# Spreading the next layer's transposes over features and token groups, and splitting rows of w2 where they are used, in a two-layer hybrid mixer

## The chip, the cores and the metric

One core of a Trainium2 chip runs the whole program in one launch. The metric is the device time of that launch in microseconds (us), from the first to the last instruction with what lies around it, as a median over runs.

## What is computed

Two layers over 512 latent tokens (X, four tiles of 128) and 256 context tokens (C, two tiles). Each layer mixes tokens and then runs a gated feed-forward network:

```python
    h = x * (1.0 + sc1) + sh1
    proj = h @ w_in[l]
    ...
    x = layer_norm(DEEPNORM_ALPHA * x + g1 * (mix @ w_out), ln1g, ln1b)
    h = x * (1.0 + sc2) + sh2
    ffn = (jax.nn.silu(h @ w1) * (h @ w3)) @ w2
    return layer_norm(DEEPNORM_ALPHA * x + g2 * ffn, ln2g, ln2b)
```

The model width D is 1024 (8 blocks of 128, called k), the feed-forward width 2816 (22 blocks of 128, called features or ft). Context tokens go through layer 0 only; layer 1 still needs their normed projections. The modulation vectors (sh, sc, g) come from `silu(c) @ w_mod[l]`.

## The kernel before

**Arithmetic.** Every fp32 operand is kept as two fp32r parts. `split` (L168, L169) writes the high part by a cast on ScalarE (ACT) and the low part by a subtraction on VectorE (DVE). `mm3` (L172 to L174) makes one product out of three matmuls.

**Weights.** A list `plan` holds every weight tile in the order of use. `getw(key, la)` returns a tile and starts the loads of the `la` tiles behind it. A plan entry made by `add` calls `wload` (L178 on): it takes one of four raw buffers (S4), one of five split buffers (W8), starts the load on SP's queue (L186), and puts the split, and for layer 1's w2 a multiplication by the gate g2 (L189), at a priority 100 steps early. An entry made by `addraw` only loads.

**Order.** A scheduler orders the instructions of each engine when the program is built, by priority and by its own estimate of when operands are ready. Each engine then works strictly through its list.

**Feed-forward, down-projection** (`wout_ffn`, from L1190). Layer 0 runs two passes over the 22 features: C0, C1, X0 in pass 0, and X1, X2, X3 in pass 1; layer 1 has one pass over the four X tiles. `feat(pi, ft)` fetches the feature's activations (`y<-yd`, L1203), gets the w2 tile and splits y into u. `mm` then multiplies, for each token tile and each half of 512 columns, so that a feature of pass 1 is 18 matmuls 128x512 with six accumulators. `fill(1)` takes one step of layer 1's modulation products (`mods`, L274: w_mod tiles of 512 KB times `sst`) in each feature.

**The hook.** At feature 6 of pass 1, `hook(res, 0)` first empties the filler down to two generators, then runs `make_h` for the context tiles over all eight k: two transposes into a PSUM buffer `ps` (L360), an activation that applies the modulation and writes `y` (L362), and the split of `y` into `hT` (u). `hook(res, 1)` does the same for X0 and X1 behind the second tile of the last features. The PS pool has four one-bank buffers; in pass 1 two are accumulators and one holds the modulation products, so one is left for the transposes.

**In-projection of layer 1** (`inproj`, L412 on). Three token groups, (C0, C1), (X0, X1), (X2, X3): the first with 160 columns, the others with 416. For each k it splits w_in, makes h of that k and multiplies. Behind a group, `make_h` of the next group's first two k (`NPRE`) follows. The accumulators are PD buffers, which also hold layer 0's last accumulators until `ffn_last` (L1021) has read them.

**Layer 1's step from up to down.** The up-projection (L1187) ends with feature 21, whose split weights wa, wb and further forms take W8 buffers too, as do the first w2 tiles.

The names in rows: `w` a W8 tile, `s` an S4 tile, `u` a split operand, `y` an unsplit one, `f` a full-width tile, `ps` and `pd` the PSUM pools PS and PD, `ident` the identity.

Of the kernel before, what the change touches and what calls it, by code (L numbers as in the profile page):

```python
# [17 lines left out]
P = 128  # L18
# [72 lines left out]
def hybrid_kernel(ctx: ExitStack, tc: tile.TileContext, out: bass.AP, g: dict):  # L91
# [233 lines left out]
    def getw(key, la=2):  # L325
        i = index[key]
        ahead(i + 1 + la)
        return ready.pop(key)
# [3 lines left out]
    def add(key, src, shape, gate=None):  # L332
        index[key] = len(plan)
        plan.append((key, lambda: wload(src, shape, gate)))
# [77 lines left out]
    def inproj(l, groups, make_h):  # L412
# [6 lines left out]
        for gi, grp in enumerate(groups):  # L419
# [8 lines left out]
            for k in range(KD):  # L428
# [7 lines left out]
                for (st, t), a in zip(grp, acc):  # L436
                    h = st.hT[k]
                    ts_ = slice(t * P, (t + 1) * P)
                    mm3(a[:, c0:NA], h[:, 0, ts_], h[:, 1, ts_], w[0][:, k % 2], w[1][:, k % 2], k == 0, k == KD - 1)
            if gi + 1 < len(groups):  # L440
                for k in range(NPRE):
                    make_h(k, groups[gi + 1])

            for i, ((st, t), ac) in enumerate(zip(grp, acc)):
# [560 lines left out]

    NCONV, NLAST = 3, 4
    DVE_LN = ((1, 1), (2, 0), (2, 1))
    gbox = []

    def ffn_last(l, st, t, accs, ya, gb, bc, final, res, tail):  # L1010

# [76 lines left out]
    def wout_ffn(l, streams, final, hook=None):  # L1088
# [103 lines left out]
        def feat(pi, ft):  # L1192

            tiles = passes[pi]
            n = len(tiles) * P
            y = Y(n)
            i = 0
            while i < len(tiles):
                st, t = tiles[i]
                c, m = col[(st.s, t)], 1  # L1200
                while i + m < len(tiles) and col[(tiles[i + m][0].s, tiles[i + m][1])] == c + m * P:
                    m += 1
                nc.sync.dma_start(out=y[:, i * P:(i + m) * P], in_=yd[l][ft][:, c:c + m * P])  # L1203
                i += m
            w2 = getw(("2", l, pi, ft), 1)
            d = U(F32R, 2 * n).rearrange("p (a b) -> p a b", a=2)
            split(d[:, 0], d[:, 1], y)
            return d, w2
# [34 lines left out]
        gb = {}  # L1243
        for ft in range(NCONV, NF):
            if ft == NF - 4:
                gb = {st.s: gates(l, 1, st.s, FT) for st in streams}
                if final:
                    gbox.append(gb[0])
            cur = unit(ft, wn)
            next(cur)  # L1250
            if ft + 1 < NF:
                wn = up_forms(l, ft + 1)
            if prev:
                next(prev)
            next(cur)
            if prev:
                next(prev)
            next(cur)
            if prev:
                run(prev)  # L1260
            prev = cur
# [12 lines left out]
        for pi, tiles in enumerate(passes):  # L1274
# [15 lines left out]
            for ft in range(NF - NLAST):  # L1290
                d = nx
                if ft + 1 < NF - NLAST:
                    nx = feat(pi, ft + 1)
                for i in range(len(tiles)):
                    mm(i, [ft], [d])
                if not final and (pi == 0 or ft < 6):
                    fill(1)
                if hook and pi and ft == 6:
                    hook(res, 0)
                if ft == 8:  # L1300
                    for st, t in tiles:
                        y = FT()
                        nc.sync.dma_start(out=y, in_=rd[l][st.jt + t])
                        G_.tensor_tensor(out=y, in0=y, in1=bc[0], op=ALU.mult)  # L1304
                        G_.tensor_tensor(out=y, in0=y, in1=bc[1], op=ALU.add)
                        ya.append(y)
            fts = list(range(NF - NLAST, NF))
            ds = [feat(pi, ft) for ft in fts]
            for i, (st, t) in enumerate(tiles):
                mm(i, fts, ds)  # L1310
                if i == len(tiles) - 1 and pi + 1 < len(passes):
                    nx = feat(pi + 1, 0)
                ffn_last(l, st, t, accs[i], ya[i], gb[st.s], lb, final, res, final and i == len(tiles) - 1)
                if hook and pi and i == 1:
                    hook(res, 1)
        return res


# [3 lines left out]
    for l in range(2):  # L1322
# [26 lines left out]
                    addraw((n, l, ft), src, (KD, P))  # L1349
        for pi in range(2 if l == 0 else 1):  # L1350
            for ft in range(NF):
                add(("2", l, pi, ft), g["w_ffn2"][l][ft * P:(ft + 1) * P, :], (D,), gbox if l == 1 else None)

    phase("inp")
    toks = {(st.s, t): I(n=D) for st, t in allg}
# [17 lines left out]
    pars = [params(0), params(1)]  # L1373
    AB = {}
    made = set()
    NPRE = 2

    def make_h(k, grp):
        if (k, grp[0]) in made:
            return  # L1380
        made.add((k, grp[0]))
        for st in (X, C):
            ts_ = [t for s_, t in grp if s_ is st]
            if not ts_:
                continue
            if len(st.hT) <= k:
                st.hT += st.alloc(1 if st.s == 0 else 2)
            sl = slice(ts_[0] * P, (ts_[-1] + 1) * P)
            to_hT([toks[(st.s, t)] for t in ts_], lambda kk: st.hT[kk][:, :, sl], *AB[st.s], ks=[k])
# [8 lines left out]
            for p in pars:  # L1398
                next(p)

    def hook(res, i):

        grp = HOOK[i]
        if not AB:
            while len(filler) > 2:
                fill(1)
            for s_ in (C, X):
                made.clear()
                AB[s_.s] = fold(1, 0, s_.s, PV[:, 0, PG2:PG2 + 8], PV[:, 0, PB2:PB2 + 8])
                s_.hT = []  # L1410
        toks.update(res)
        for k in range(KD):
            make_h(k, grp)

    HOOK = [allg[4:6], allg[0:2]]
    for st in (X, C):
        st.hT = []
    AB.update({st.s: (modT[:, 0, 1, st.s], modT[:, 0, 0, st.s]) for st in (X, C)})
# [96 lines left out]
```

## Time and profile before

| | us |
|---|---|
| median of 3 runs | 1672.93 |
| lowest and highest run | 1671.89, 1675.65 |
| the profiled execution's own time | 1668.66 |
| its span, first to last instruction | 1666.9 |
| PE (TensorE) busy | 1572.3 (94%) |
| DVE busy | 1045.8 (63%) |
| ACT busy | 769.3 (46%) |
| POOL (GpSimd) busy | 260.6 (16%) |
| mean granted clock of TensorE, share of full | 0.984 |

A timeline row has the start, the duration, the engine (SPq is SP's queue), the program line, the operation, what is written from what, how many instructions of the kind follow one another, and in brackets the idle time before with what ended it. Each engine's idle time can be asked for any stretch; PE is the one that fills the span, so its idle rows are the places where another engine sets the time. PEclk of a window is the mean granted clock as a share of 2.4 GHz; 0.5 is the level of 1.2 GHz. Places used below, in us of the span: layer 0's pass 0, 752 to 882; pass 1, 882 to 1004; layer 1's in-projection, 1004 to 1036; layer 1's up-projection until 1519 and its down-projection from there.

### The profile page before, as it was taken

The page shows a single profiled execution, that of the slowest core. Times are in us where ns is not written, and L with a number is a line of the kernel's source. Part 1 is how long each engine was busy: PE and PEld are TensorE (multiplying, and loading weights), DVE is VectorE, ACT ScalarE, POOL GpSimd, SP SyncE. Part 2 cuts the span into 40 slices and gives each one's busy share as a digit, 9 for nine tenths or more (in the row PEclk, how much of TensorE's full clock was granted, in tenths as well). Part 3 has the DMA queues.
Part 4 walks back from the last instruction along what each step waited for, and adds up shares of the span by engine and source line. Part 5 has one row for each costly group of instructions (what it writes and reads, how often), then busy time and mean ns, then how long its engine had stood idle before and what let it go on. Part 6 is the DMA issues. An engine that isn't in the chain of part 4 may idle for free.

```text
span 1666.9 us, 23834 instructions
## 1 busy us (share of the span) xinstructions
PE 1572.3 (94%) x9129; PEld 1358.9 (82%) x9129; DVE 1045.8 (63%) x1591; ACT 769.3 (46%) x1371; POOL 260.6 (16%) x322
## 2 busy tenths in 40 slices
PE   6999889999999999999999798989999899998997
PEld 3856778888899999997766487879988899997786
DVE  1443676876766666664544437677857778886835
ACT  2521675884633434344232516368845445554220
POOL 0213011330000000000305005433311000001402
PEclk9999999999999999999999799999999999999999
DMA  9566114128322333449876726411156244457321
GB/s 327 178 218 202 39 39 140 46 81 279 110 82 93 94 95 101 130 133 338 315 257 226 222 67 200 145 33 39 39 176 197 76 127 127 127 177 266 119 82 58
DMA packets 180502, 241.80 MB, mean 145 GB/s; under 512 B 10874, under 2 KB 127468, under 8 KB 180388
## 3 DMA queue, kind: packets, MB, share of 16 engines
q1 hardware_dynamic: 180388, 240.28, 44.8%
q8 instruction: 72, 1.18, 0.3%
q14 instruction: 42, 0.34, 0.1%
HBM read 215.30 MB, written 24.94 MB: 144 GB/s over the span
## 4 chain that ended last, share of the span: by engine, by line
PE 81%; DVE 8%; DMA 4%; ACT 4%; issue 2%; SPq 0%; POOL 0%; POOLq 0%; DVEq 0%; ACTq 0%
PE pd L1187 21%; PE pd L172 10%; PE pd L173 10%; PE pd L174 10%; PE ps L172 5%; PE ps L173 5%; PE ps L174 5%; PE ps L1187 4%; PE ps L274 3%; PE ps L731 3%; PE ps L715 2%; DVE w L169 2%; DVE u L169 2%; DMA u<-in_w_mod_dram 1%; DMA s<-in_w_ffn_dram 1%
## 5 line engine op out<-in xcount | busy, mean ns | idle before, releaser
L168 ACT CAST w<-s 128x1024 fp32r<-128x1024 f32 (+3 forms) x285 | 292.7, 1031 | 473.0 <-PE pd L1187 141.2
L169 DVE TENSOR_TENSOR w<-s,w 128x1024 fp32r<-128x1024 f32 (+3 forms) x285 | 352.5, 1244 | 195.8 <-ACT w L168 195.7
L1187 PE MATMUL pd<-u,w 128*128 128x256 f32 (+1 forms) x1938 | 295.4, 308 | 19.0 <-DVE w L169 14.3
L1187 PEld LDWEIGHTS pd<-u,w 128*128 128x128 f32 x1938 | 282.7, 191 | 25.2 <-DVE w L169 15.8
L172 PE MATMUL pd<-w,u 128*128 128x512 f32 (+5 forms) x728 | 277.9, 383 | 8.3 <-DVE u L169 3.6
L173 PE MATMUL pd<-w,u 128*128 128x512 f32 (+5 forms) x728 | 274.3, 377 | 1.7 <-DVE w L169 1.7
L174 PE MATMUL pd<-w,u 128*128 128x512 f32 (+5 forms) x728 | 272.9, 376 | 0.0
L172 PEld LDWEIGHTS pd<-w,u 128*128 128x128 f32 x728 | 140.3, 193 | 54.6 <-issue 16.3
L173 PEld LDWEIGHTS pd<-w,u 128*128 128x128 f32 x728 | 140.3, 193 | 29.3 <-issue 5.9
L174 PEld LDWEIGHTS pd<-w,u 128*128 128x128 f32 x728 | 140.2, 193 | 27.2 <-issue 4.2
L168 ACT CAST u<-y 128x512 fp32r<-128x512 f32 (+2 forms) x178 | 94.2, 546 | 61.5 <-DMA y<-yd 28.4
L169 DVE TENSOR_TENSOR u<-y,u 128x512 fp32r<-128x512 f32 (+2 forms) x118 | 77.7, 679 | 63.0 <-ACT u L168 61.8
L169 POOL TENSOR_TENSOR u<-y,u 128x512 fp32r<-128x512 f32 (+1 forms) x60 | 78.9, 1323 | 225.5 <-ACT u L168 203.2
L172 PE MATMUL ps<-u,w 128*128 128x256 f32 (+2 forms) x288 | 92.1, 328 | 1.8 <-DVE modT L300 1.1
L174 PE MATMUL ps<-u,w 128*128 128x256 f32 (+2 forms) x288 | 93.5, 327 | 0.0
L173 PE MATMUL ps<-u,w 128*128 128x256 f32 (+2 forms) x288 | 93.3, 326 | 0.1
L172 PE MATMUL ps<-w,u 128*128 128x512 f32 (+1 forms) x208 | 81.2, 398 | 5.6 <-DVE u L169 4.7
L169 DVE TENSOR_TENSOR u<-ps,u 128x512 fp32r<-128x512 f32 (+2 forms) x106 | 66.7, 654 | 28.8 <-ACT u L168 27.8
L173 PE MATMUL ps<-w,u 128*128 128x512 f32 (+1 forms) x208 | 82.0, 395 | 1.4 <-DVE w L169 1.4
L174 PE MATMUL ps<-w,u 128*128 128x512 f32 (+1 forms) x208 | 81.4, 393 | 0.0
L1304 POOL TENSOR_TENSOR f<-f,f 128x1024 f32<-128x1024 f32 x10 | 25.8, 2598 | 333.5 <-DMA f<-rd 254.4
L1187 PE MATMUL ps<-u,w 128*128 128x384 f32 (+1 forms) x456 | 75.3, 313 | 0.0
(250 smaller groups left out, 2579.5 us busy)
## 6 DMA issues: line engine op xcount, KB each, us to landing
s<-in_w_ffn_dram SPq DMA_DIRECT2D x154, 512.0 KB
s<-in_w_out_dram SPq DMA_DIRECT2D x50, 512.0 KB
u<-in_w_mod_dram SPq DMA_DIRECT2D x48, 512.0 KB
s<-in_w_mod_dram SPq DMA_DIRECT2D x48, 512.0 KB
s<-in_w_in_dram SPq DMA_DIRECT2D x16, 512.0 KB
yd<-f SPq DMA_DIRECT2D x19, 384.0 KB
y<-yd SPq DMA_DIRECT2D x88, 64.0 KB
y<-yd SPq DMA_DIRECT2D x22, 256.0 KB
```

The lines of the kernel that those rows point to most:

```text
L168: A_.copy(out=hi, in_=src)
L169: (eng or V_).tensor_tensor(out=lo, in0=src, in1=f(hi), op=ALU.subtract)
L172: T_.matmul(ps, lhsT=ll, rhs=rh, start=start, stop=False)
L173: T_.matmul(ps, lhsT=lh, rhs=rl, start=False, stop=False)
L174: T_.matmul(ps, lhsT=lh, rhs=rh, start=False, stop=stop)
L274: T_.matmul(ps[32 * j:32 * j + 32, :n], lhsT=sst[:, k, :], rhs=ws[j // 2][:, (j % 2) * n:(j % 2 + 1) * n], start=(k == 0), stop=(k == KD - ...
L715: T_.transpose(pt[:, o:o + P], es[t2][:, k * P:(k + 1) * P], ident)
L731: T_.matmul(av[:, 0:256], lhsT=vt[k][:, h, :], rhs=pts[k // 2][:, a, (k % 2) * 256:(k % 2 + 1) * 256], start=(k == 0 and a == 1), stop=(k ...
L1187: T_.matmul(ps, lhsT=A[u][:, k], rhs=B[k][:, v], start=first and k == 0 and i == 0, stop=last and k == 3 and i == 2, skip_group_check=True)
L1304: G_.tensor_tensor(out=y, in0=y, in1=bc[0], op=ALU.mult)
```

## The change

1. **w2 raw.** w2's plan entries become raw loads, two tiles ahead (one for the last two features). `feat` takes the W8 buffer itself, multiplies by the gate where it is layer 1, and splits, at normal priority. `gbox` goes.
2. **Hook per feature.** In features 5 to 12 of pass 1 the hook is called with k = ft - 5 and makes that k of C0, C1 and X0: a pair of transposes for C and a single one for X0. The call behind the second tile goes.
3. **Filler.** It takes a step in a feature only while more than one generator is left, so that the last one, `mods(1, (4, 5))`, keeps its other steps for layer 1.
4. **In-projection.** h of the next group is made inside the loop over k, one k each; `made` remembers k and tile, so X1 is made alone (X0 being there) and the pair (X2, X3) behind the multiplications of the same k.

```diff
--- before.py
+++ after.py
@@ -437,8 +437,7 @@
                     h = st.hT[k]
                     ts_ = slice(t * P, (t + 1) * P)
                     mm3(a[:, c0:NA], h[:, 0, ts_], h[:, 1, ts_], w[0][:, k % 2], w[1][:, k % 2], k == 0, k == KD - 1)
-            if gi + 1 < len(groups):
-                for k in range(NPRE):
+                if gi + 1 < len(groups):
                     make_h(k, groups[gi + 1])
 
             for i, ((st, t), ac) in enumerate(zip(grp, acc)):
@@ -1005,7 +1004,6 @@
 
     NCONV, NLAST = 3, 4
     DVE_LN = ((1, 1), (2, 0), (2, 1))
-    gbox = []
 
     def ffn_last(l, st, t, accs, ya, gb, bc, final, res, tail):
 
@@ -1202,7 +1200,12 @@
                     m += 1
                 nc.sync.dma_start(out=y[:, i * P:(i + m) * P], in_=yd[l][ft][:, c:c + m * P])
                 i += m
-            w2 = getw(("2", l, pi, ft), 1)
+            s2 = getw(("2", l, pi, ft), 2 if ft < NF - 2 else 1)
+            w2 = W8()
+            if final:
+                V_.tensor_tensor(out=s2, in0=s2, in1=gb[0], op=ALU.mult)
+            split(w2[:, 0, :D], w2[:, 1, :D], s2)
+            w2 = w2[:, 0, :D], w2[:, 1, :D]
             d = U(F32R, 2 * n).rearrange("p (a b) -> p a b", a=2)
             split(d[:, 0], d[:, 1], y)
             return d, w2
@@ -1243,9 +1246,7 @@
         gb = {}
         for ft in range(NCONV, NF):
             if ft == NF - 4:
-                gb = {st.s: gates(l, 1, st.s, FT) for st in streams}
-                if final:
-                    gbox.append(gb[0])
+                gb.update({st.s: gates(l, 1, st.s, FT) for st in streams})
             cur = unit(ft, wn)
             next(cur)
             if ft + 1 < NF:
@@ -1293,10 +1294,11 @@
                     nx = feat(pi, ft + 1)
                 for i in range(len(tiles)):
                     mm(i, [ft], [d])
-                if not final and (pi == 0 or ft < 6):
-                    fill(1)
-                if hook and pi and ft == 6:
-                    hook(res, 0)
+                if hook:
+                    if len(filler) > 1:
+                        fill(1)
+                    if pi and 5 <= ft < 5 + KD:
+                        hook(res, ft - 5)
                 if ft == 8:
                     for st, t in tiles:
                         y = FT()
@@ -1311,8 +1313,6 @@
                 if i == len(tiles) - 1 and pi + 1 < len(passes):
                     nx = feat(pi + 1, 0)
                 ffn_last(l, st, t, accs[i], ya[i], gb[st.s], lb, final, res, final and i == len(tiles) - 1)
-                if hook and pi and i == 1:
-                    hook(res, 1)
         return res
 
 
@@ -1349,7 +1349,7 @@
                     addraw((n, l, ft), src, (KD, P))
         for pi in range(2 if l == 0 else 1):
             for ft in range(NF):
-                add(("2", l, pi, ft), g["w_ffn2"][l][ft * P:(ft + 1) * P, :], (D,), gbox if l == 1 else None)
+                addraw(("2", l, pi, ft), g["w_ffn2"][l][ft * P:(ft + 1) * P, :].rearrange("p (a n) -> p a n", a=2), (2, 512))
 
     phase("inp")
     toks = {(st.s, t): I(n=D) for st, t in allg}
@@ -1373,14 +1373,10 @@
     pars = [params(0), params(1)]
     AB = {}
     made = set()
-    NPRE = 2
-
     def make_h(k, grp):
-        if (k, grp[0]) in made:
-            return
-        made.add((k, grp[0]))
         for st in (X, C):
-            ts_ = [t for s_, t in grp if s_ is st]
+            ts_ = [t for s_, t in grp if s_ is st and (k, s_.s, t) not in made]
+            made.update((k, st.s, t) for t in ts_)
             if not ts_:
                 continue
             if len(st.hT) <= k:
@@ -1398,21 +1394,18 @@
             for p in pars:
                 next(p)
 
-    def hook(res, i):
-
-        grp = HOOK[i]
+    def hook(res, k):
+
         if not AB:
-            while len(filler) > 2:
+            while len(filler) > 1:
                 fill(1)
             for s_ in (C, X):
                 made.clear()
                 AB[s_.s] = fold(1, 0, s_.s, PV[:, 0, PG2:PG2 + 8], PV[:, 0, PB2:PB2 + 8])
                 s_.hT = []
         toks.update(res)
-        for k in range(KD):
-            make_h(k, grp)
-
-    HOOK = [allg[4:6], allg[0:2]]
+        make_h(k, allg[4:6] + allg[0:1])
+
     for st in (X, C):
         st.hT = []
     AB.update({st.s: (modT[:, 0, 1, st.s], modT[:, 0, 0, st.s]) for st in (X, C)})
```

Up to PE's instruction of about 740 us the two programs' orders are the same on every engine. Three places differ in what matters here.

PE, pass 1 before, the hook: rows of its list from the last matmul of feature 6 (`w_1265`) to the first of feature 7 (`w_1271`); `f_7403` and `f_7407` are the normed context tiles, `f_7411` is X0.

```order
L174 MATMUL pd_7935<-w_1265_8143,u_8184 128x512
L360 MATMUL ps_8244<-ident,f_7403 128x128
L360 MATMUL ps_8244<-ident,f_7407 128x128
L360 MATMUL ps_8251<-ident,f_7403 128x128
L360 MATMUL ps_8251<-ident,f_7407 128x128
L360 MATMUL ps_8259<-ident,f_7403 128x128
L360 MATMUL ps_8259<-ident,f_7407 128x128
L360 MATMUL ps_8266<-ident,f_7403 128x128
L360 MATMUL ps_8266<-ident,f_7407 128x128
L360 MATMUL ps_8722<-ident,f_7411 128x128
L172 MATMUL ps_7932<-w_1271_8180,u_8281 128x512
```

PE, pass 1 of the change: the last matmul of one feature, five transposes in three PSUM tiles, and the first matmul of the next.

```order
L174 MATMUL pd_7934<-w_1257_8111,u_8114 128x512
L360 MATMUL ps_8151<-ident,f_7402 128x128
L360 MATMUL ps_8151<-ident,f_7406 128x128
L360 MATMUL ps_8188<-ident,f_7410 128x128
L360 MATMUL ps_8194<-ident,f_7402 128x128
L360 MATMUL ps_8194<-ident,f_7406 128x128
L172 MATMUL ps_7931<-w_1269_8163,u_8166 128x512
L173 MATMUL ps_7931<-w_1269_8163,u_8166 128x512
```

The long run of context pairs at one place is gone. In its stead, behind eight features, stand by turns one transpose (X0) and five (a context pair, X0 of the next k, its context pair); the five stand four times.

ACT, pass 1 of the change, beside those five transposes; `w_1310` is a later feature's w2, `u_8166` the high part of the feature that PE takes next.

```order
L168 CAST w_1310_8349<-s_1287_8248 128x1024
L362 ACTIVATE y_8154<-ps_8151,ab_8135 128x256
L168 CAST u_8150<-y_8154 128x256
L362 ACTIVATE y_8190<-ps_8188,ab_8139 128x128
L168 CAST u_8166<-y_8158 128x384
L168 CAST u_8187<-y_8190 128x128
L362 ACTIVATE y_8197<-ps_8194,ab_8135 128x256
L168 CAST u_8150<-y_8197 128x256
L168 CAST u_8209<-y_8201 128x384
```

The cast of a w2 tile stands ahead of the activation that frees the transposes' buffer, and the high part of the next feature stands between two such activations.

DVE, layer 1, end of the up-projection, before: `w_2185` is the split of wa of feature 21, `w_2182` and `w_2184` are w2 of features 0 and 1, `s_2183` and `s_2207` raw w2 tiles.

```order
L169 TENSOR_TENSOR w_2182_14141<-s_2181_14140,w_2182_14141 128x1024
L169 TENSOR_TENSOR u_14569<-y_14561,u_14569 128x512
L169 TENSOR_TENSOR u_14604<-y_14596,u_14604 128x512
L189 TENSOR_TENSOR s_2183_14146<-s_2183_14146,f_13867 128x1024
L1233 TENSOR_TENSOR f_13991<-f_13991,f_13992 128x256
L189 TENSOR_TENSOR s_2207_14388<-s_2207_14388,f_13867 128x1024
L169 TENSOR_TENSOR w_2184_14147<-s_2183_14146,w_2184_14147 128x1024
L1236 TENSOR_TENSOR f_13992<-f_13992,pd_13989 128x256
L1237 TENSOR_TENSOR f_13991<-f_13991,f_13992 128x256
L169 TENSOR_TENSOR w_2185_14152<-s_2170_14020,w_2185_14152 128x1024
```

The same place in the change; wa is `w_2199`, `w_2191` the form that stands ahead of it in both.

```order
L1206 TENSOR_TENSOR s_2197_14180<-s_2197_14180,f_13907 128x1024
L169 TENSOR_TENSOR f_14198<-y_14187,f_14198 128x512
L169 TENSOR_TENSOR w_2191_14075<-s_2175_13940,w_2191_14075 128x1024
L169 TENSOR_TENSOR w_2199_14184<-s_2186_14060,w_2199_14184 128x1024
L169 TENSOR_TENSOR u_14502<-y_14494,u_14502 128x512
L1232 TENSOR_TENSOR f_14032<-f_14032,pd_14029 128x256
L169 TENSOR_TENSOR u_14537<-y_14529,u_14537 128x512
L169 TENSOR_TENSOR u_14572<-y_14564,u_14572 128x512
```

Before, two gate multiplications and the split of w2's second tile stand between `w_2182` and wa's split; now wa's split follows directly behind `w_2191`, and of w2 only the first gate multiplication stands ahead of both.

## Rows read from the trace of the kernel before

**Rows 1.** The page, part 1: engine, busy us, share, instructions.
```profile
PE 1572.3 (94%) x9129; PEld 1358.9 (82%) x9129; DVE 1045.8 (63%) x1591; ACT 769.3 (46%) x1371; POOL 260.6 (16%) x322
```

**Rows 2.** Waits of PE, 880 to 1110 us: total us, times, longest.
```profile
PE ps L360 <- ACT y L362: 8.4, 6, 3.2
```

**Rows 3.** PE timeline at the hook: start, us, engine line op, idle before.
```profile
929.03 0.44 PE L360 MATMUL ps<-ident,f 128*128 128x128 f32 x2 [1.20 <-ACT y L362]
932.72 0.69 PE L360 MATMUL ps<-ident,f 128*128 128x128 f32 x2 [3.25 <-ACT y L362]
...
937.12 0.48 PE L360 MATMUL ps<-ident,f 128*128 128x128 f32 x1 [0.66 <-ACT y L362]
942.25 0.80 PE L172 MATMUL ps<-w,u 128*128 128x512 f32 x1 [4.65 <-DVE u L169]
```

**Rows 4.** SP timeline, 915 to 942 us: the queue's issues and waits.
```profile
919.32 15.89 SPq L186 DMA_DIRECT2D s<-in_w_ffn_dram  x9
935.27 5.63 SPq L1203 DMA_DIRECT2D y<-yd  x8
```

**Rows 5.** ACT timeline, 927 to 943 us.
```profile
927.47 1.05 ACT L168 CAST w<-s 128x1024 fp32r<-128x1024 f32 x1 [1.67 <-DMA s<-in_w_ffn_dram]
928.42 0.56 ACT L362 ACTIVATE y<-ps,ab 128x256 f32<-128x256 f32 x1
929.01 0.41 ACT L168 CAST u<-y 128x256 fp32r<-128x256 f32 x1
...
941.09 2.11 ACT L168 CAST u<-y 128x384 fp32r<-128x384 f32 x4 [3.59 <-DMA y<-yd]
```

**Rows 6.** DVE timeline, 927 to 943 us.
```profile
941.63 1.60 DVE L169 TENSOR_TENSOR u<-y,u 128x384 fp32r<-128x384 f32 x3 [3.67 <-ACT u L168]
```

**Rows 7.** Windows: span, busy us of PE, PEld, DVE, ACT, POOL; PEclk, DMA share.
```profile
943.00:950.00 7.00, 7.00 (x22) 5.53 (x21) 3.59 (x7) 3.43 (x7) 0.00 (x0) 0.64 0.65 187
1009.00:1020.00 11.00, 8.48 (x35) 7.70 (x35) 11.00 (x16) 5.99 (x12) 5.51 (x6) 0.69 0.60 187
1028.00:1036.00 8.00, 6.09 (x28) 3.79 (x28) 6.14 (x12) 4.85 (x18) 6.07 (x6) 1.00 0.79 260
1496.00:1500.00 4.00, 1.35 (x12) 1.15 (x11) 4.00 (x7) 3.66 (x8) 0.00 (x0) 1.00 0.73 223
1512.00:1520.00 8.00, 7.67 (x40) 7.54 (x41) 6.23 (x10) 4.28 (x8) 0.00 (x0) 0.62 0.46 159
```

**Rows 8.** PE timeline between the in-projection's groups.
```profile
1011.09 0.46 PE L172 MATMUL pd<-w,u 128*128 128x416 f32 x1 [0.79 <-DVE f L1021]
...
1013.61 0.71 PE L173 MATMUL pd<-w,u 128*128 128x416 f32 x1 [1.73 <-DVE w L169]
...
1027.67 0.90 PE L360 MATMUL ps<-ident,f 128*128 128x128 f32 x4 [1.59 <-ACT y L362]
1028.67 1.05 PE L274 MATMUL ps<-s,sst 128*32 128x512 f32 x4
1031.51 0.46 PE L172 MATMUL pd<-w,u 128*128 128x416 f32 x1 [1.79 <-DVE u L169]
```

**Rows 9.** PE timeline, layer 1, from up- to down-projection.
```profile
1499.06 3.10 PE L1187 MATMUL pd<-u,w 128*128 128x256 f32 x24 [2.65 <-DVE w L169]
...
1512.33 2.93 PE L1187 MATMUL pd<-u,w 128*128 128x256 f32 x12 [5.92 <-DVE w L169]
```

**Rows 10.** DVE timeline, the same stretch.
```profile
1499.86 1.28 DVE L169 TENSOR_TENSOR u<-y,u 128x512 fp32r<-128x512 f32 x2
...
1507.99 1.22 DVE L189 TENSOR_TENSOR s<-s,f 128x1024 f32<-128x1024 f32 x1 [3.04 <-DMA s<-in_w_ffn_dram]
...
1511.06 1.22 DVE L169 TENSOR_TENSOR w<-s,w 128x1024 fp32r<-128x1024 f32 x1
```

**Rows 11.** DVE timeline, from 1540 us.
```profile
1542.05 3.42 DVE L189 TENSOR_TENSOR s<-s,f 128x1024 f32<-128x1024 f32 x1
```

**Rows 12.** POOL timeline, from 1530 us.
```profile
1541.00 6.69 POOL L1305 TENSOR_TENSOR f<-f,f 128x1024 f32<-128x1024 f32 x2
```

## Prediction

> **What bounds the kernel now.** I read the page first: PE is busy for 94% of the span [rows 1], so time can come only from where PE stands idle or runs at the lower clock. Then the waits of PE by stretch, then the timelines of PE at those places, and at each the engine that PE waited for. The programs are alike up to about 740 us, and from there to 929 us PE has no idle stretch over 0.25 us; layer 0's step from up- to down-projection, though its w2 loads change too, has nothing to give. Three places are left.
>
> *Pass 1, the hook.* PE makes context transposes through one free PSUM buffer, so each pair waits until ACT has read the pair before [rows 2]. In the run of pairs PE is idle 1.20, 3.25, 1.02, 0.66 and 0.66 us (the third and fourth lie between the rows shown) and then 4.65 us for the next feature's tokens [rows 3]: 11.4 us. The 4.65 goes back to SP's queue: it stood 15.89 us in nine issues of w2 loads, with the token fetches behind them [rows 4], and ACT got its tokens only at 941.09 [rows 5]. Afterwards the granted clock is 0.64 over 943 to 950 [rows 7]; 0.36 x 7 us is 2.5 us lost at the 1.2 GHz level. Sum: 14 us.
>
> *Between the in-projection's groups.* Idle 0.79, 1.73, 1.59 and 1.79 us [rows 8], and a clock of 0.69 over 1009 to 1020 [rows 7]: 0.31 x 11 is 3.4 us, of which 0.9 lies in idle time already counted. Sum: 5.9 + 2.6, some 8.5 us.
>
> *Layer 1, from up to down.* Idle 2.65 and 5.92 us for a weight's split on DVE [rows 9], then a clock of 0.62 over 1512 to 1520 [rows 7], 3.0 us, of which 0.2 is idle time: 11.4 us. The 5.92 comes from order: wa's split on DVE (the row at 1511.06) stands behind a gate multiplication that waited 3.04 us for its w2 load [rows 10].
>
> **The hook per feature.** All of the 14 us can go: SP's list has one w2 load and one token fetch per feature, and the long run of pairs is gone. What comes instead are four runs of five transposes in three PSUM tiles, still through one buffer. From ACT's list: the cast of a w2 tile starts when the feature's last matmul has freed its W8 buffer, 1.05 us; then the activation of the first pair, 0.56; only then X0's transpose; the cast of the next feature's tokens, 0.53 (2.11 for four), behind X0's activation, which I put at 0.45 between the 0.41 and the 0.56 of the rows beside it [rows 5]; then that feature's low part on DVE, 0.53 [rows 6], which PE needs. With the hand-overs between engines that is about 3.5 us from the last matmul of one feature to the first of the next, where the transposes alone would take some 0.5. So 3.0 us lost at each, **12.4 us with four**, counting 0.1 more each for the single transposes in between. Bounds: two waits of 0.66 us, as where ACT had nothing else [rows 3], give 1.3 each and 5 in all; a DMA wait as in the 3.25 would give 5 each and 20 in all. I take the middle one, since the cast ahead is in the list.
>
> Does the clock fall in these runs? Rows point both ways. After 1.20 and 3.25 us of idle time among transposes it fell [rows 3, 7], and after 0.79 and 1.73 too; after 1.59 and 1.79 with seven transposes and four modulation matmuls among them, at 1028 to 1036, it stayed at 1.00, and after 2.65 us at 1.00 as well [rows 7, 8, 9]. A fall costs 2.5 to 2.8 us as above. I count four in ten: 4 x 0.4 x 2.6, 4.2 us. The Trainium skill, "TensorE: Matmul & The Clock Gate", Part 4 on PE-mode transposes, says that transposes do not count as PE activity for the gate; by it all four runs look idle and the sum would be 10.4 us in place of 4.2. Whether these rows are of that mode the trace does not tell, and the 1.00 at 1028 to 1036 speaks against it.
>
> Pass 1: 14 - 12.4 - 4.2, **2.6 us slower**.
>
> **The filler.** Seven steps of `mods(1, (4, 5))` leave pass 1 and come in layer 1: 28 matmuls at 1.05 / 4 us [rows 8] are some 7 us of PE's work moved from one place to another, which counts nothing. Their 14 loads of 512 KB meet the w_in loads there, where the DMA share is already 0.79 [rows 7]. They are interleaved with them in SP's list and fit a free buffer ring by my estimate; bounds nothing and 4 us (an S4 buffer late twice, 1.7 us each as ACT's waits for a load [rows 5]). I take **1 us**.
>
> **In-projection.** X1 alone is transposed beside group 0's matmuls, and X2, X3 beside group 1's, so most of the idle time at 1027 and 1031 has other work to lie behind. But eleven transposes still come in one run ahead of group 2, through ACT: 1.5 us. And DVE's list now has the read of layer 0's last accumulators (L1021), for which group 1 waits, behind group 0's evacuation, a w_in split and two splits of tokens: about 2.9 us in place of 0.79 + 1.73. ACT and DVE get 8 activations, 8 casts and 8 low parts more (X1 no longer shares them with X0): 8 x (0.45 + 0.4) is 7 us on ACT, in pass 1's and this stretch's free time, not on the path. With a clock fall as likely as not, 2.9 + 1.5 + 1.3, 5.7 remain of 8.5: **2.8 us faster**; bounds 0 and 6.
>
> **w2 raw.** wa's split follows the split before it in DVE's list. So the 5.92 us and the clock's 2.8 after it go, while the 2.65, behind the first gate multiplication, stays. What is late next is the split of w2's first tile. From the row at 1499.06 PE has 108 matmuls ahead of its first use, at 3.10 / 24 us each [rows 9] 14.0 us. DVE has six full-width operations (1.22 each), nine of half the width (0.64, by 1.28 for two) and six of a quarter (0.3) [rows 10]: 14.9 us, and if a gate's load is late once more, 1 to 2 more. PE thus waits 1 to 3 us there. Of the 8.7 that go, 2.1 comes back, and another 1 is lost further on, where DVE is behind as before: **5.5 us faster**. Bounds: 0, if all of it is waited for later, and 9.
>
> **Sum.** -2.6 + 2.8 + 5.5 - 1 = 4.7 us faster than the profiled execution's 1668.66. That execution is 4.3 us below the median of the three runs, 1672.93; against the median I predict 1672.93 - 4.7, **1668 us**. A measurement of this kernel can tell some 0.2%, 3.3 us, from no change.
>
> **Rivals.**
>
> *A, the five transposes are hidden.* If ACT keeps up (its token cast early, the w2 cast done before the feature's last matmul), each run of five costs 1 us and no clock. For it: ACT stands idle at the hook until loads land, 1.67 and 3.59 us [rows 5], so it has time to spare. Against: one buffer, and the lists' order. 14 - 4 + 2.8 + 5.5 - 1 is 17 us, 1656 us.
>
> *B, the clock falls at every run of five.* Place: features 5 to 12 of pass 1. Each costs 3.1 + 2.6, 22.8 us for four against the 14 that go; with the filler's loads late by 4 us, 1 us gained between groups and 5 at w2, the program is 7 us **slower**, 1680. It decides from three falls on: then pass 1 alone loses 6.2 us. The drops to 0.64 and 0.69 after idle times among transposes [rows 7] speak for it. The Trainium skill, same page, section on PSUM-queue depth-cycling, tells of the same mechanism: PE idles briefly between groups as buffers cycle, and the clock goes down and up with them; the two drops agree with it, the 1.00 at 1028 to 1036 does not.
>
> *C, the wait at wa is only moved.* DVE is the engine behind from 1496 us on, and at 1542 one gate multiplication takes 3.42 us beside POOL's residual work (6.69 us for two) against 1.22 elsewhere [rows 10, 11, 12]. If the stretch up to w2's sixth tile is bound by DVE's total work, what PE gains at wa it waits for behind it, all but the gate's 3.04 us on DVE: about 3 us remain instead of 5.5, and with pass 1 at -2.6, the in-projection at 2 and the loads at -2 the sum is nothing: 1673.
>
> *D, the programs differ, but not where it counts:* the scheduler's lists have the change in them at all three places, so I give this none of its own.
>
> **How the numbers follow.** Forecast 0.38, A 0.15, C 0.24, B 0.23. The forecast's own bounds, with its pass 1 between 0.4 falls more and less and w2 between 3 and 8, are 1664 to 1671. The range over cases goes from A's 1656 down by its price's uncertainty of 1 to B's 1680: 1655 to 1680; it leaves out half of A's and of B's outer halves, 0.19. Faster: A, and nearly all of the forecast's part below 1669.6 (0.35): 0.50. Same: C and the rest of the forecast: 0.26. Slower: B and a little of C: 0.24.
>
> **What would show it.** Right: four waits of PE for ACT's L362 of about 1.2 and 0.6 us, and one for a token's low part, behind features 5 to 12, and no wait of 4 us at the next token fetch; no PE wait over 1 us at wa near 1512, a wait of 1 to 3 us at the first w2 matmul; SP's w_mod loads in layer 1 without PE waiting at L274. Wrong: granted clock below 0.8 at three or four of those features (B); hardly any L360 wait (A); waits on DVE of 5 us and more between w2's first and sixth feature (C); L274 waiting for `s<-in_w_mod` in layer 1.

## The result and the profile after

The change is **slower**: 1682.15 us (median of five runs, 1679.33 to 1683.32) against 1671.89 (1670.63 to 1675.65), a ratio of 1.0056 with a 95% interval of 1.0044 to 1.0069, some 10 us. It lies above the range of the prediction, and on the other side of no change than forecast. Ratios here and below are to the kernel before, timed again beside each run, so they and not the medians are compared between runs. The profiled execution has a span of 1680.4 us against 1666.9.

The page's part 1 of the change, which answers to [rows 1]:

```profile
PE 1578.2 (94%) x9129; PEld 1363.7 (81%) x9129; DVE 1059.5 (63%) x1599; ACT 771.7 (46%) x1387; POOL 271.3 (16%) x322
```

PE is busy for as large a share as before of a longer span. Its waits from 880 to 1110 us (columns as in [rows 2]):

```profile
PE ps L360 <- ACT y L362: 9.3, 9, 1.6
PE ps L274 <- DMA s<-in_w_mod_dram: 6.4, 2, 3.9
...
PE ps L360 <- ACT f L1040: 3.4, 2, 2.9
```

In this stretch [rows 2] had six waits of 8.4 us for ACT's L362; now there are nine of 9.3 us (one of about 1.6 us lies between the layers in both), and two kinds of wait that did not exist: for w_mod's loads, and for `f`, a normed token tile. PE's timeline behind the features (as [rows 3]), the first two of the four runs of five transposes:

```profile
908.48 0.38 PE L360 MATMUL ps<-ident,f 128*128 128x128 f32 x2
910.24 0.33 PE L360 MATMUL ps<-ident,f 128*128 128x128 f32 x1 [1.38 <-ACT y L362]
911.12 0.44 PE L360 MATMUL ps<-ident,f 128*128 128x128 f32 x2 [0.55 <-ACT y L362]
913.86 0.80 PE L172 MATMUL ps<-w,u 128*128 128x512 f32 x1 [2.30 <-DVE u L169]
...
926.79 0.33 PE L360 MATMUL ps<-ident,f 128*128 128x128 f32 x1 [1.38 <-ACT y L362]
927.67 0.44 PE L360 MATMUL ps<-ident,f 128*128 128x128 f32 x2 [0.55 <-ACT y L362]
928.68 0.50 PE L172 MATMUL ps<-w,u 128*128 128x512 f32 x1 [0.57 <-DVE u L169]
```

Each run shows the two waits that the prediction had worked out, 1.38 and 0.55 us, and a third for the next feature's tokens, 2.30 at the first and some 0.57 at the others. At the first, the tokens' low part stood on DVE behind a w2 split of 3.25 us (at 909.75). The 4.65 us wait of [rows 3] is gone; the long issue of [rows 4] has become a shorter one of four loads:

```profile
894.46 13.21 SPq L341 DMA_DIRECT2D s<-in_w_ffn_dram  x4
```

The granted clock (windows, as [rows 7]), behind each of the four runs and then between the in-projection's groups:

```profile
913.00:919.00 6.00, 5.14 (x12) 4.08 (x13) 1.90 (x5) 0.72 (x2) 0.00 (x0) 0.50 0.41 122
930.00:933.00 3.00, 3.00 (x9) 2.31 (x8) 0.56 (x1) 0.51 (x1) 0.00 (x0) 0.50 0.35 127
944.00:946.50 2.50, 2.50 (x8) 1.93 (x7) 0.56 (x1) 0.51 (x1) 0.00 (x0) 0.50 0.28 94
957.50:960.00 2.50, 2.50 (x7) 1.91 (x7) 0.11 (x1) 0.51 (x1) 0.00 (x0) 0.50 0.93 303
1005.00:1036.00 31.00, 21.96 (x81) 16.88 (x82) 22.25 (x28) 14.97 (x34) 14.49 (x13) 0.67 0.61 200
1025.00:1035.00 10.00, 7.47 (x22) 4.46 (x21) 4.40 (x10) 4.58 (x12) 0.00 (x0) 0.50 0.82 261
```

It fell to 1.2 GHz behind all four runs of pass 1, and its mean was 0.67 over the 31 us between the in-projection's groups, where [rows 7] had one window of 0.69 and then 1.00. PE's timeline there, answering to [rows 8]:

```profile
1003.82 0.33 PE L360 MATMUL ps<-ident,f 128*128 128x128 f32 x1 [1.61 <-ACT y L362]
1007.03 0.90 PE L360 MATMUL ps<-ident,f 128*128 128x128 f32 x3 [2.88 <-ACT f L1040]
...
1023.84 1.92 PE L274 MATMUL ps<-s,sst 128*32 128x512 f32 x4 [3.91 <-DMA s<-in_w_mod_dram]
...
1029.77 1.92 PE L274 MATMUL ps<-s,sst 128*32 128x512 f32 x4 [2.53 <-DMA s<-in_w_mod_dram]
```

Waits of 0.79 to 1.79 us have become 1.61, 2.88, 3.91 and 2.53. And from up- to down-projection, answering to [rows 9]:

```profile
1514.44 1.68 PE L1185 MATMUL pd<-u,w 128*128 128x256 f32 x12 [2.68 <-DVE w L169]
...
1523.14 1.69 PE L1185 MATMUL pd<-u,w 128*128 128x256 f32 x12 [1.37 <-ACT f L1235]
...
1553.11 0.50 PE L173 MATMUL ps<-w,u 128*128 128x512 f32 x1 [2.20 <-DVE w L169]
...
1573.60 0.80 PE L173 MATMUL ps<-w,u 128*128 128x512 f32 x1 [4.25 <-DVE w L169]
```

The 2.65 us stayed (2.68), the 5.92 at wa became 1.37, and behind it stand two waits for the split of w2, 2.20 and 4.25, where before had 2.19 (for `f`, L1236) and 1.43. From 1490 to 1580 us PE's idle time went from 13.1 to 11.3 us.

Where the time went, added up from PE's timeline between the same matmuls of every program (a missing record shifts a bound by some tenths; "idle" is the sum of the brackets, "modulation" the time from an L274 row to the next row without its wait, "half clock" what 128x512 and 128x416 matmuls took over their full-clock spacing of 0.23 and 0.19 us):

| profiled execution | pass 1: length, idle, half clock, modulation | between the layers: length, idle, modulation | from there into layer 1's down-projection |
|---|---|---|---|
| before | 122.6, 11.4, 2.6, 10.8 | 103.1, 8.4, 4.0 | 460.2 |
| the change | 117.7, 11.7, 6.6, 2.0 | 126.6, 17.7, 13.6 | 457.8 |
| e3 (raw w2 alone) | 119.6, 7.2, 1.8, 11.8 | 114.4, 16.0, 6.7 | 452.7 |
| e6 (e3, no load ahead) | 120.8, 8.0, 2.0, 11.8 | 104.4, 9.3, 4.7 | 455.5 |
| e7 (the change, no load ahead) | 116.7, 10.9, 6.3, 2.0 | 118.1, 11.1, 12.8 | 458.5 |
| e9 (e6, pairs by feature) | 110.2, 2.1, 0.0, 11.8 | 104.7, 8.4, 4.9 | 453.9 |
| e12 (e6, the change's hook) | 130.5, 13.6, 5.8, 11.8 | 107.0, 11.2, 3.9 | 452.0 |

So the change loses between the layers, even with the modulation steps that moved there (8.8 us out of pass 1, 9.6 in) taken off: 23.5 - 9.6, some 14 us, while pass 1 without them is 3.9 us longer and layer 1 2.4 us shorter. One execution can lie some us from its kernel's median, so places are read here and sizes from the ratios.

### The profile page after: what moved, and what is told of

Its sections match the earlier page's. It is cut to its first block, busy times and chain, and to the rows that moved or that the text cites. A ratio compares the mean times of both kernels' runs of the same rounds, so it can differ in the third digit from the quotient of the medians.

```text
span 1680.4 us, 23893 instructions
## 1 busy us (share of the span) xinstructions
PE 1578.2 (94%) x9129; PEld 1363.7 (81%) x9129; DVE 1059.5 (63%) x1599; ACT 771.7 (46%) x1387; POOL 271.3 (16%) x322
## 4 chain that ended last, share of the span: by engine, by line
PE 78%; DVE 8%; DMA 5%; ACT 4%; issue 3%; POOL 1%; SPq 0%; POOLq 0%; DVEq 0%; ACTq 0%
PE pd L1185 21%; PE pd L172 10%; PE pd L173 9%; PE pd L174 9%; PE ps L172 5%; PE ps L173 5%; PE ps L174 5%; PE ps L1185 4%; PE ps L274 3%; PE ps L730 3%; PE ps L714 2%; DVE w L169 2%; DVE u L169 2%; DMA s<-in_w_ffn_dram 2%; ACT w L168 1%
## 5 line engine op out<-in xcount | busy, mean ns | idle before, releaser
L168 ACT CAST w<-s 128x1024 fp32r<-128x1024 f32 (+2 forms) x285 | 292.4, 1030 | 472.3 <-PE pd L1185 142.3
L169 DVE TENSOR_TENSOR w<-s,w 128x1024 fp32r<-128x1024 f32 (+2 forms) x285 | 366.6, 1292 | 188.8 <-ACT w L168 184.6
L168 ACT CAST u<-y 128x512 fp32r<-128x512 f32 (+3 forms) x186 | 95.7, 530 | 60.4 <-DMA y<-yd 41.8
L169 DVE TENSOR_TENSOR u<-y,u 128x512 fp32r<-128x512 f32 (+3 forms) x126 | 77.8, 638 | 59.8 <-ACT u L168 59.5
L173 PE MATMUL ps<-w,u 128*128 128x512 f32 (+1 forms) x208 | 83.6, 402 | 6.8 <-DVE w L169 6.8
L172 PE MATMUL ps<-w,u 128*128 128x512 f32 (+1 forms) x208 | 81.7, 401 | 4.0 <-DVE u L169 4.0
L174 PE MATMUL ps<-w,u 128*128 128x512 f32 (+1 forms) x208 | 83.2, 400 | 0.0
L1185 PE MATMUL pd<-u,f 128*128 128x384 f32 (+1 forms) x456 | 74.0, 312 | 0.0
```

The source lines that it names most:

```text
L168: A_.copy(out=hi, in_=src)
L169: (eng or V_).tensor_tensor(out=lo, in0=src, in1=f(hi), op=ALU.subtract)
L172: T_.matmul(ps, lhsT=ll, rhs=rh, start=start, stop=False)
L173: T_.matmul(ps, lhsT=lh, rhs=rl, start=False, stop=False)
L174: T_.matmul(ps, lhsT=lh, rhs=rh, start=False, stop=stop)
L1185: T_.matmul(ps, lhsT=A[u][:, k], rhs=B[k][:, v], start=first and k == 0 and i == 0, stop=last and k == 3 and i == 2, skip_group_check=True)
```

## The experiments

Two theories stood first: the moved modulation steps wait for their loads (1), or making the next group's h inside the loop holds the groups up (2). Each was undone alone in the change, and w2's part was taken alone and undone.

**e1, the filler's rule of before in the change.**

```diff
-                    if len(filler) > 1:
+                    if pi == 0 or ft < 6:
                         fill(1)
```

> The change, with the filler's rule of before alone put back: in pass 1 the features 0 to 5 take a modulation step again, so those loads and products are done before the in-projection. Theory 1 (the moved w_mod loads come late between the in-projection's groups): the waits of PE at L274 for in_w_mod, 3.9 + 2.5 us, go, and with them most of the half clock at 1020 to 1035; 8 to 12 us faster than the change, 1670 to 1674. Theory 2 (making the next group's h inside the loop over k delays the groups): the wait of 2.9 us at L360 for L1040 and the low clock after it stay; at most 3 us faster than the change, 1679 or more.

Measured 1681.49 us, ratio 1.0063 (1.0042 to 1.0084): no gain. Two waits at L274 for in_w_mod, 3.3 and 2.6 us, are still there, with only the two steps in layer 1 that before had. Theory 1 falls: the number of the loads is not what makes them late.

**e2, the in-projection of before in the change** (the next group's first two k behind the group).

```diff
-                if gi + 1 < len(groups):
-                    make_h(k, groups[gi + 1])
+            if gi + 1 < len(groups):
+                for k in range(2):
+                    make_h(k, groups[gi + 1])
```

> The change, with the next group's h made behind the group again (its first two k), the rest of each k ahead of its multiplication. Theory 2: the waits at L360 before group 1 (1.6 + 2.9 us) and the clock's fall go, 6 to 9 us faster than the change, 1673 to 1676. Theory 1: they were only the first to be late, the w_mod loads are as late as before; within 3 us of the change, 1679 to 1685.

1682.07 us, 1.0059 (1.0039 to 1.0079). Theory 2 falls too: the waits only changed their names (5.2 us for a copy of group 0's accumulators, then 2.8, 2.1 and 3.4).

**e3, raw w2 alone on the kernel before** (`addraw` and the lines in `feat`, as in the change's diff).

> The kernel before with w2 fetched raw and split at its feature, nothing else. The prediction's term for it was 5.5 us faster than before, 1666. The trace of the change shows its lag shrink by only 2 us between 1500 and 1560, so by the rival that the wait is only moved (DVE bound) it is 1 to 3 us, 1669 to 1671, with waits on w's split behind the first w2 features.

1669.62 us, 0.9996 (0.9981 to 1.0012): nothing. But the table shows a sum of three: pass 1 gains 3 us, layer 1 gains 7.5, and the stretch between the layers, which this part was not thought to touch, loses 11.

**e4, w2 loaded ahead again in the change.**

> The change with w2 loaded, gated and split ahead as before. If the parts add, it is slower than the change by what e3 gains on the kernel before: 5.5 us (1688) by the prediction's term, 1 to 3 us (1683 to 1685) if the wait is only moved. If it is faster than the change, w2's split at normal priority costs pass 1 something that the waits at L1187 hide.

1681.65 us, 1.0068 (1.0047 to 1.0089), as slow as the change. So raw w2 is worth nothing in both surroundings, and the rest of the change costs some 10 us in both.

**What raw w2 does between the layers.** SP's timeline before, from the last w2 loads on (L186 issues w_in here, L1047 writes X1's residual):

```profile
972.53 15.76 SPq L186 DMA_DIRECT2D s<-in_w_in_dram  x5
1002.58 0.34 SPq L1047 DMA_DIRECT2D xn<-f  x1
1004.93 9.01 SPq L186 DMA_DIRECT2D s<-in_w_in_dram  x4
```

and in the change (L1045 is that write):

```profile
965.82 34.55 SPq L186 DMA_DIRECT2D s<-in_w_in_dram  x8
1000.42 0.46 SPq L1045 DMA_DIRECT2D xn<-f  x1
1001.53 12.81 SPq L186 DMA_DIRECT2D s<-in_w_in_dram  x5
...
1019.02 8.21 SPq L260 DMA_DIRECT2D s<-in_w_mod_dram  x4
```

Five w_in loads stood ahead of the write, now eight. What follows is DVE's order, in the change

```profile
1000.50 1.00 DVE L169 TENSOR_TENSOR w<-s,w 128x832 fp32r<-128x832 f32 x1
...
1002.15 0.97 DVE L169 TENSOR_TENSOR w<-s,w 128x832 fp32r<-128x832 f32 x1
1003.44 1.03 DVE L169 TENSOR_TENSOR w<-s,w 128x832 fp32r<-128x832 f32 x1 [0.32 <-ACT w L168]
...
1005.12 1.02 DVE L169 TENSOR_TENSOR w<-s,w 128x832 fp32r<-128x832 f32 x1
...
1006.47 1.28 DVE L1019 TENSOR_TENSOR f<-pd,f 128x512 f32<-128x512 f32 x2
```

and before:

```profile
1009.76 1.27 DVE L1021 TENSOR_TENSOR f<-pd,f 128x512 f32<-128x512 f32 x2
...
1012.54 1.01 DVE L169 TENSOR_TENSOR w<-s,w 128x832 fp32r<-128x832 f32 x1
```

Before, the read of X3's accumulators (L1021, here L1019) came ahead of every split of group 1's w_in (128x832), now it comes behind four; ACT has the casts of these ahead of X2's normalisation (L1040) likewise, and PE waited 2.88 us for that. That the scheduler took those splits to be ready first is the likely reason; no run shows its estimate. w_mod's loads need raw buffers that the w_in splits free: SP issues them at 1019.02, 24 us behind pass 1's last matmul, against 20 before (1023.96). Four splits ahead of that read were in the list of the change, of e1 and e2, and of e3. The order vanished from the lists in two ways, which were then run: raw w2 in layer 1 alone, and raw w2 everywhere with no load started ahead of the last feature's w2. (That line acts at the end of pass 0 and of layer 1 too; the table has its gain between the layers.)

**e5, raw w2 in layer 1 alone.**

```diff
+            if final:
+                s2 = getw(("2", l, pi, ft), 2 if ft < NF - 2 else 1)
...
+            else:
+                w2 = getw(("2", l, pi, ft), 1)
```

> The kernel before with w2 fetched raw in layer 1's down-projection alone; layer 0 loads and splits it ahead as before. Theory 3 (raw w2 in layer 0 changes the lists at the layer's end: the splits of w_in of group 1 come ahead of the read of X3's accumulators on DVE and of X2's normalisation on ACT, 10 to 11 us; in layer 1 it saves 7 us): the in-projection is as before, 6 to 8 us faster than before, 1662 to 1664. Rival (the 7 us in layer 1 are only what PE catches up after having come late): no gain in layer 1, within 2 us of before.

1666.72 us, 0.9976 (0.9963 to 0.9989): 4 us faster, the in-projection as before. That lies between the theory and its rival: a gain, but not the 7.5 us of e3's last column. Measured as in the table, e5's is 457.3, 2.9 us less than before; so part of e3's 7.5 may be PE catching up, as the rival held.

**e6, raw w2 in both layers, no load ahead of the last one.**

```diff
-            s2 = getw(("2", l, pi, ft), 2 if ft < NF - 2 else 1)
+            s2 = getw(("2", l, pi, ft), 2 if ft < NF - 2 else NF - 1 - ft)
```

> The kernel before with w2 raw in both layers, but no load is started ahead of the last feature's w2 (in the change the first w_in tile is, and takes its split buffer there). The lists of DVE and ACT between the layers have the order of before again. Theory 3: the loss of 10 to 11 us between the layers goes, 1662 to 1664. Rival (the loss comes from raw w2 itself, splits at normal priority late in pass 1): it stays, 1668 to 1671.

1662.41 us, 0.9951 (0.9937 to 0.9966), as theory 3 said, and 7.5 us better than e3 by the ratios. DVE has the old order again:

```profile
1007.59 1.28 DVE L1020 TENSOR_TENSOR f<-pd,f 128x512 f32<-128x512 f32 x2
...
1010.37 1.01 DVE L169 TENSOR_TENSOR w<-s,w 128x832 fp32r<-128x832 f32 x1
```

**e7, the same line in the whole change.**

> The whole change, but no load is started ahead of the last feature's w2. Theory 3: about 10 us faster than the change, 1669 to 1673, the waits at L360 for L1040 and at L274 for in_w_mod shorter as in the kernel with w2 put back (0.8, 1.4 and 1.2 us). Rival (the transposes and modulation steps moved into this stretch are what delays it): no more than 3 us faster than the change, 1677 or more.

1671.79 us, 1.0010 (0.9997 to 1.0023): 7.7 us better than the change by the ratios, and the same as before. Theory 3 holds in both surroundings: one argument, the number of loads started ahead, was worth 7 to 8 us. What is left against e6, 10 us, is hook, filler and in-projection.

**e8, e5 and one pair of context transposes in each of the features 2 to 9.**

> The kernel before with w2 raw in layer 1 alone and one pair of context transposes in each of the features 2 to 9 of pass 1; X0 and X1 as before at the end of the pass. If the single transpose buffer costs time only where two groups meet in one feature, no wait at L360 over 0.5 us is left in pass 1 and most of the 14 us go as well: 1650 to 1656. If the token fetches behind w2 loads in SP's queue were the cause, 4 to 5 us of waits on the tokens stay.

1662.79 us, 0.9952 (0.9935 to 0.9968). The waits at L360 went down to one of 0.7 us, but two waits for a token's low part, 4.3 and 2.8 us, stayed. Only the second is the outcome that the expectation named: SP issued those tokens at 943.10, behind seven w2 loads of 11.27 us. The first is DVE's: two context low parts ahead of it took 5.17 us (at 906.72), beside POOL's residual work.

**e9, e6 with one pair in each of the features 6 to 13.**

```diff
-                if hook and pi and ft == 6:
-                    hook(res, 0)
+                if hook and pi and 6 <= ft < 6 + KD:
+                    hook(res, 0, [ft - 6])
```

> The best kernel so far (w2 raw in both layers, no load ahead of the last feature's w2; hook and in-projection as before) with one pair of context transposes in each of the features 6 to 13 of pass 1 in place of all eight at feature 6. Its ratio so far is 0.995. Theory 4 (waits at L360 come only where two groups of transposes meet): the 7 us of waits at the hook go and with them the clock's fall of 2 to 3 us, 1651 to 1656. Rival (each pair waits for a cast of w2 on ACT, wherever it stands): one wait of 1 us at each pair is left, and it is no more than 3 us faster than the best so far, 1660 to 1664.

**1649.76 us, 0.9876 (0.9856 to 0.9897): 1.2% faster than before, the fastest of all**, and better than theory 4 had said. PE's waits for these two in pass 1 and at its end are now

```profile
PE ps L172 <- DVE u L169: 1.5, 2, 0.9
...
PE ps L360 <- ACT y L362: 0.7, 1, 0.7
```

and the half clock in pass 1 is gone (table). Against e12 below, e9 also leaves X0 to the end of the pass and starts one feature later.

**e10, e6 with the change's filler alone** (diff as in the change).

> The same best kernel with the change's filler alone: five modulation steps go from pass 1 to layer 1. Theory 5 (they wait there for w_mod, and where a step's two tiles stand apart it costs PE 1.96 us in place of 0.99): 1 to 4 us slower than the best so far, 1664 to 1667, a wait at L274 for in_w_mod over 1 us before group 2. Rival (the work is only moved): within 1 us, 1661 to 1664.

1663.39 us, 0.9956 (0.9939 to 0.9974): within 1 us of e6, the rival's outcome, and no wait at L274 over 0.5 us. The work is only moved.

**e11, e6 with the change's in-projection alone.**

> The same best kernel with the change's in-projection alone: the next group's h is made inside the loop over k. The prediction had 2.8 us faster for it (1660). By the pair of kernels with and without it on the whole change it is worth 0 to 2 us slower, 1662 to 1665.

1661.29 us, 0.9944 (0.9926 to 0.9962): about 1 us faster than e6, less than the interval can tell.

**e12, e6 with the change's hook alone.**

> The same best kernel with the change's hook alone: C0, C1 and X0 of one k in each of the features 5 to 12. Theory 4: four waits of 1.4 + 0.6 + 0.6 us or more in pass 1 as in the change, against 8 us of waits now, and between the layers one w_in split more ahead of X3's accumulators; 3 to 8 us slower than the best so far, 1666 to 1671. Rival (the hook is neutral and the loss of the change is the filler's and the in-projection's): 1660 to 1664.

1673.70 us, 1.0026 (1.0012 to 1.0040): 12.5 us slower than e6 by the ratios, more than theory 4 allowed. PE's timeline in pass 1, some of its waits:

```profile
924.88 0.33 PE L360 MATMUL ps<-ident,f 128*128 128x128 f32 x1 [1.89 <-ACT y L362]
928.33 0.80 PE L172 MATMUL ps<-w,u 128*128 128x512 f32 x1 [3.12 <-DVE u L169]
...
944.84 0.33 PE L360 MATMUL ps<-ident,f 128*128 128x128 f32 x1 [1.38 <-ACT y L362]
945.72 0.54 PE L360 MATMUL ps<-ident,f 128*128 128x128 f32 x2 [0.55 <-ACT y L362]
...
974.04 0.80 PE L172 MATMUL ps<-w,u 128*128 128x512 f32 x1 [3.72 <-DVE u L169]
```

The pattern of the change is here (1.38, 0.55), with waits of 3 us for tokens beside it; idle time and half clock in pass 1 are 19.4 us against e6's 10.0, and 2.6 us are added between the layers, where one w_in split stands ahead of the read of X3's accumulators again (at 1013.0). So of the change's rest the hook is the one that costs; filler and in-projection are neutral.

## Why the prediction was wrong

By the ratios, against before: raw w2 alone gains nothing, and 8 us without the load ahead; hook, filler and in-projection together 10 to 11 us slower in three surroundings (e4; the change and e3; e7 and e6). The prediction had 5.5 us faster and 0.8 us slower for the two.

**The step that failed first** stands in the first paragraph: that "layer 0's step from up- to down-projection, though its w2 loads change too, has nothing to give". That reading is of one step, but the sum has no term for raw w2 in layer 0 at all; it prices it in layer 1 alone. In layer 0 it does two things. At the old hook it takes 4 to 5 of the 14 us by itself (pass 1's idle time and half clock, 14.0 before, 9.0 in e3, 10.0 in e6); the prediction had booked these to the hook. In e6:

```profile
940.27 0.79 PE L172 MATMUL ps<-w,u 128*128 128x512 f32 x1 [0.97 <-DVE u L169]
...
919.65 14.59 SPq L341 DMA_DIRECT2D s<-in_w_ffn_dram  x8
```

The wait for tokens is 0.97 us in place of 4.65. It is not that SP was free earlier: eight w2 loads held it for 14.59 us and it issued the tokens at 935.66, against 935.27 before [rows 4]. But seven of the eight context pairs now stand in one run ahead of the next feature on PE, where before had five, and the wait for the tokens' landing lies behind them; that feature's first matmul also starts 2 us sooner (940.27 against 942.25), and what shortened the fetch stays open. And raw w2 shifts the lists at the layer's end, which costs 7 to 8 us. The lists were read there, and the read of X3's accumulators behind a w_in split was named, but as the in-projection's doing and at 2.9 us. It is not the in-projection's: e2 has the four splits without it, and e11 none with it. One split comes with the hook (e4, e7, e12), the others with the load ahead (e6 and e7).

**The hook.** The waits came where and as they were worked out: four runs of 4.2, 2.5, 2.5 and 2.5 us make 11.7 against 12.4. The clock's term was mis-sized: 4.2 us, from four falls in ten at 2.6 us. The clock fell behind all four runs, and 6.6 us (table) is 1.65 us for each, so that two errors went against each other. Nor does such a run always bring a fall: in e2, with the same waits of 1.38 and 0.55 us at all four, it fell behind the first and the third, and behind the second and the fourth it did not:

```profile
928.00:938.00 10.00, 8.90 (x39) 7.02 (x39) 2.86 (x6) 3.95 (x8) 0.00 (x0) 1.00 0.41 122
...
955.00:965.00 10.00, 9.51 (x40) 7.48 (x41) 3.80 (x8) 4.28 (x9) 0.00 (x0) 1.00 0.68 199
```

Waits and clock together are 18.3 for the 14.0 of before, so 4.3 us slower instead of 2.6. Against e6, where only 10 us were left to win, that is 8 or 9. e12's own trace has 9.4 us more than e6's in pass 1 and 2.6 between the layers; no run parts the order there from the clock. The Trainium skill's sentence on transposes ("TensorE: Matmul & The Clock Gate", Part 4: PE-mode transpose), that they do not count as busy time for the clock in the same way, would let all four runs bring a fall. The trace of the change agrees in that, e2's does not; whether these transposes are of that mode no run shows.

**The filler**, 1 us slower: e10 has 0.8 us, but that is luck, for the late loads that the 1 us was for did not come there. Five steps moved, not seven: two of the eight stood in layer 1 before. The waits for w_mod in the change are mostly the load ahead's doing (they are 3.9 and 2.5 us there, 1.5 and 1.0 in e7). **The in-projection**, 2.8 us faster: 1 us (e11), which the intervals cannot tell from nothing, and nothing on the change (e2).

**w2 in layer 1.** The 5.92 us did go. The half clock behind it only came later (the last row below), and the wait was not 1 to 3 us once but 2.20 and 4.25: rival C's mechanism, in part. DVE's splits there, and the clock behind the second wait:

```profile
1549.66 3.39 DVE L169 TENSOR_TENSOR w<-s,w 128x1024 fp32r<-128x1024 f32 x1
...
1562.19 9.09 DVE L169 TENSOR_TENSOR u<-y,u 128x512 fp32r<-128x512 f32 x4
...
1572.34 1.21 DVE L169 TENSOR_TENSOR w<-s,w 128x1024 fp32r<-128x1024 f32 x1
...
1572.00:1578.00 6.00, 4.40 (x10) 3.47 (x11) 6.00 (x7) 2.61 (x3) 0.00 (x0) 0.50 0.49 129
```

Beside POOL's residual work (1547 to 1570 us) one split of w2 took 3.39 us and four low parts 9.09; behind it a split took 1.21 and a low part 0.68. In the change the stretch in the table's last column gained 2.4 us, in e3 and e6 7.5 and 4.7. e5, the only run with raw w2 in layer 1 alone, measured 4.0 (1.8 to 6.2), so that the 5.5 was of the right size, if high.

**The rivals.** A fell with the rows at 910 and 911. B named the right sign and nearly the right time (1680), and its sign came: the clock fell behind all four runs. But it had 22.8 us for these runs and 18.3 were measured, and the half clock is 4 us more than before, of 10; it was not the cause of most. C is the layer-1 part. No rival held the loss between the layers.

## What to carry to other kernels

Where a scheduler orders the engines, a change of when buffers are taken and loads are started has to be followed to the next stage's first reads of PSUM: a few splits of the next weights, ready early, that stand ahead of the read which frees an accumulator, cost 7 to 8 us here, more than the 5.92 us wait that the change took away. One PSUM buffer is enough to hide transposes if each stretch of matmuls has one group of them; two groups in one stretch waited for ACT in turn (1.38 and 0.55 us) and mostly paid at the clock as well. And test the parts of a bundled change apart: here one part won 8 us, one lost 12, and a single argument, the number of loads started ahead, hid the first.

## What was not expected of the hardware

A modulation step multiplies two w_mod tiles, each into its own 32-column groups of the array. PE's timeline before, one step with its two tiles together and one tile alone:

```profile
886.11 1.06 PE L274 MATMUL ps<-s,sst 128*32 128x512 f32 x8
...
890.53 1.05 PE L274 MATMUL ps<-s,sst 128*32 128x512 f32 x4
```

Eight records take 1.06 us and four take 1.05. A tile apart from its partner costs as much as both, so where the order parts them, as in pass 1 before, a step takes about 2 us: the six steps there take 10.8 us (table). The prediction's price of 1.05 us for four listed products holds for the step that stays together.
